# Weight, x, y and m tiles moved to multiples of 64 bytes in a hybrid-mixer and FFN kernel

## The chip, the cores and the metric

The kernel runs on one core of a Trainium2 chip, in one launch. The metric is the device time of that core in microseconds (us), the median of several runs. All times below come from those runs or from one execution taken by the hardware profiler.

## What is computed

Two blocks follow each other on one sequence of 256 tokens, 1024 wide, all in float32. The first has a mixer (an RG-LRU branch, a gated linear attention, a block attention with relative bias), then a SwiGLU FFN, each with RMS norms. The second has two layers, both modulated by a condition vector `c`: a short convolution with an FFN, then an attention with forget gates and an FFN. Cut to the part that fills the time:

```python
def first_block(x, ...):
    h = rms_norm(x, pre_mix_norm)
    x = x + rms_norm(hybrid_mixer(h, w_in, ...) @ w_out, post_mix_norm)
    h = rms_norm(x, pre_ffn_norm)
    f = (silu(h @ w_ffn_gate) * (h @ w_ffn_up)) @ w_ffn_down
    return x + rms_norm(f, post_ffn_norm)

def second_block(x, c, ...):
    for l in range(2):
        sh1, sc1, g1, sh2, sc2, g2 = split(silu(c) @ w_ada[l] + b_ada[l], 6)
        h = x * (1 + sc1) + sh1
        y = short_conv_mixer(h, ...) if l == 0 else forgetting_attention(h, ...)
        x = layer_norm(ALPHA * x + g1 * y, ...)
        h = x * (1 + sc2) + sh2
        y = (silu(h @ w_gate[l]) * (h @ w_up[l])) @ w_down[l]
        x = layer_norm(ALPHA * x + g2 * y, ...)
    return x
```

The widths are 1024 for the model and 2816 (22 tiles of 128) inside the FFNs.

## The kernel before

**Layout.** Activations are kept transposed: a tile is 128 features on the partitions by 256 tokens along the row, and the 1024 features are NK = 8 such k tiles. Weights come as blocks of 128 x 128; eight blocks make one `raw` tile of 1024 columns, loaded by one 512 KB transfer on the SP queue (`raw_load`).

**Two halves.** TensorE multiplies in fp32r. To keep float32's accuracy every operand is split in two: a rounded high part and the rest as a low part. For weights `weights` does it (ScalarE writes `wh`, L140; VectorE writes `wl`, L144), for operands `hilo`, `modulate`, `deep_norm` and the end of `evac` in `ffn`. Each product is then three matmuls: high by high, low weight by high operand, high weight by low operand (`mm3`, L151 to L153). The weight block is the stationary operand, the operand tile of 256 columns the moving one.

**The operand tiles.** `hl_tiles` makes the x tiles (`xh`, `xl`) and the y tiles (`yh`, `yl`), eight of each kind in pools that live through the whole program. They are T + 2 = 258 columns wide: in `lazy` two further columns, for the scale and shift of a layer norm, go through the same matmuls, and everywhere else only the first 256 are used. The m tiles (`mh`, `ml`, the inner values of an FFN, 22 of each) are made in `ffn` (L888, L889), also 258 columns wide, of which the first 256 are used.

**Order of the matmuls.** `single` and `pair` go over k inside one output tile: three matmuls on k tile 0, three on k tile 1, and so on (`mm3`). `ksteps` (L186 to L192, under `kouter`, `partial` and `lazy`) goes over k outside: one x or y high tile meets four to eight weight blocks in a row, high and low weight in turn, then its low tile meets the high weights. A down projection (`single` with 22 k tiles) does the same as other singles over m tiles. `tokmajor` (L240 to L242) has the operand as the stationary side and 256 or 512 weight columns as the moving one, and `small_proj` (L468, L469) uses 16 or 32 columns of a small weight tile `w_glrs` or `w_fs`.

**What sets the order.** A scheduler places the instructions of each engine by a simulated timeline, bound by the dependencies that `after` adds. `fill` puts a share of the 112 modulation products (`gemv`, a 512 KB transfer and one VectorE instruction each, L360) between the projections.

**Where tiles lie.** Pools are laid out one behind the other along the row of a partition; a tile's row is rounded up to a multiple of 32 bytes, so 258 columns of 4 bytes, 1032, take 1056. The first pool, `const`, holds the constants made in `consts`; behind it come `raw`, `whp`, `wlp`, `gp`, `xp` and the rest.

The placing lines before:

```python
w = T + 2                                              # hl_tiles, L247
h = self.tl(pool or self.xp, [P, w], tag + "h", F32R, NK)
h = self.tl(self.fp, [P, T + 2], "mh", F32R)[:, 0:T]   # ffn, L888
```

Of the kernel before, what the change touches and what calls it, by code (L numbers as in the profile page):

```python
# [10 lines left out]
F32R = mybir.dt.float32r  # L11
# [6 lines left out]
P = 128  # L18
D = 1024
T = 256  # L20
# [43 lines left out]
class Net:  # L64
# [42 lines left out]

    def ms(self, shape=(P, 512)):
        return self.tl(self.pms, list(shape), "ms")

    def acc(self, shape=(P, 512)):
        return self.tl(self.pacc, list(shape), "acc")
# [131 lines left out]

    def hl_tiles(self, tag, pool=None):

        w = T + 2  # L247
        h = self.tl(pool or self.xp, [P, w], tag + "h", F32R, NK)
        l = self.tl(pool or self.xp, [P, w], tag + "l", F32R, NK)
        return h, l, h[:, 0:T], l[:, 0:T]  # L250

    def hilo(self, src, tag="x", scale=None, pool=None):
# [126 lines left out]
    def consts(self):  # L379
        nc, cp, a = self.nc, self.cp, self.a  # L380
        self.vt = self.tl(cp, [P, NVEC], "vec")
        nc.scalar.dma_start(self.vt, a["vec"])
        self.x0 = []
        self.early = []
        for i in range(NK // 2):
            t = self.tl(self.sp, [P, 2, T], "ax", bufs=NK // 2)
            nc.sync.dma_start(t, a["xT"][i])
            self.x0 += [t[:, 0, :], t[:, 1, :]]
            if i < EARLY:
                self.early.append(self.raw_load(i, 4 if i == 0 else 2))  # L390
        self.ct = self.tl(cp, [P, NCST], "cst")
        nc.sync.dma_start(self.ct, a["cst"])
        self.odim = self.tl(cp, [P, P], "odim")
        nc.gpsimd.memset(self.odim, 1.0 / D)
        self.rdim = self.tl(cp, [P, 1], "rdim")
        nc.vector.memset(self.rdim, 1.0 / D)
        self.ident = self.tl(cp, [P, P], "ident")
        make_identity(nc, self.ident)
        self.tbl = self.tl(cp, [P, 1], "tbl")
        nc.vector.memset(self.tbl, 0.0)  # L400
        nc.scalar.activation(self.tbl, self.tbl, AF.Exp)
        self.G = self.tl(cp, [P, T], "fG", BF16)
        nc.gpsimd.memset(self.G, 0.0)
        self.fsel = self.tl(cp, [P, 16], "fsel", BF16)
        nc.gpsimd.memset(self.fsel, 0.0)
        for o in (0, 32, 64):
            nc.vector.tensor_copy(self.fsel[o:o + 16, :], self.ident[o:o + 16, o:o + 16])
        self.fneg = self.tl(cp, [P, 16], "fneg", BF16)
        nc.vector.tensor_scalar(self.fneg, self.fsel, -1.0, None, ALU.mult)
        self.identb = self.tl(cp, [P, P], "identb", BF16)  # L410
        nc.vector.tensor_copy(self.identb, self.ident)
        self.cmask = self.tl(cp, [P, P], "cmask", BF16)
        cm = self.tmp("p_sq")[:, 0:P]
        nc.gpsimd.memset(cm, 0.0)
        nc.gpsimd.affine_select(out=cm, in_=cm, compare_op=ALU.is_ge, fill=NEG, base=0,
                                pattern=[[-1, P]], channel_multiplier=1)
        nc.vector.tensor_copy(self.cmask, cm)
        self.gmask = self.tl(cp, [P, P], "gmask")
        nc.gpsimd.memset(self.gmask, 1.0)
        nc.gpsimd.affine_select(out=self.gmask, in_=self.gmask, compare_op=ALU.is_ge, fill=0.0, base=0,  # L420
                                pattern=[[1, P]], channel_multiplier=-1)
        nc.gpsimd.memset(self.gmask[0:64, 64:128], 0.0)
        self.hmask = self.tl(cp, [P, 4], "hmask")
        nc.gpsimd.memset(self.hmask, 0.0)
        self.bmask = self.tl(cp, [P, 4, 64], "bmask")
        nc.gpsimd.memset(self.bmask, 0.0)
        for h in range(4):
            nc.gpsimd.memset(self.hmask[32 * h:32 * h + 32, h:h + 1], 1.0)
            nc.gpsimd.memset(self.bmask[32 * h:32 * h + 32, h, :], 1.0)
        self.hsel = self.tl(cp, [P, 2], "hsel")  # L430
        nc.gpsimd.memset(self.hsel, 0.0)
        for h in range(2):
            nc.gpsimd.memset(self.hsel[64 * h:64 * h + 64, h:h + 1], 1.0)
        self.resetm = self.tl(cp, [P, 4, 64], "resetm")
        nc.gpsimd.memset(self.resetm, 1.0)
        nc.gpsimd.memset(self.resetm[:, :, 0:1], 0.0)
        cst = lambda name, n, rows=P: self.ct[0:rows, COFF[name]:COFF[name] + n]
        self.rel = cst("rel_bias", 8, 32)
        self.oh = cst("onehot", T, 32)
        self.gw2 = cst("gate_w2", P, 32)  # L440
        self.fold = cst("fold", 16, 32)
        self.bf = cst("b_f", 1, 16)
        self.wbd = [cst(n, 2 * P).rearrange("p (t c) -> p t c", t=2) for n in ("lru_wa", "lru_wx")]
        self.wsm = []
        for name in ("w_glr", "w_f"):
            r = cst(name, P).rearrange("p (k c) -> p k c", k=NK)
            w = self.tl(cp, [P, NK, 2, 16], name + "s", F32R)
            nc.scalar.activation(w[:, :, 0, :], r, AF.Copy)
            nc.vector.tensor_tensor(w[:, :, 1, :], r, w[:, :, 0, :].bitcast(F32), ALU.subtract)
            self.wsm.append(w)  # L450
        self.ada = self.tl(cp, [P, 112], "ada")

    def silu_c(self):
        nc, ca = self.nc, self.a["c"]
        self.cact = self.tl(self.cp, [P, D], "cact")
        cb = self.tl(self.gp, [P, D], "gw")
        nc.sync.dma_start(cb, bass.AP(tensor=ca.tensor, offset=ca.offset, ap=[[0, P], [1, D]]))
        nc.scalar.activation(self.cact, cb, AF.Tanh, scale=0.5)
        nc.vector.scalar_tensor_tensor(cb, self.cact, 1.0, cb, op0=ALU.add, op1=ALU.mult)
        nc.vector.tensor_scalar(self.cact, cb, 0.5, None, ALU.mult)  # L460
# [408 lines left out]
    def ffn(self, l, X, R=None, R2=None, first=(), rows=None):  # L869

        nc = self.nc
        V = nc.vector
        MH, ML = [], []

        def evac(g, u):
            if R is not None:
                g2 = self.tmp("ff_g")
                V.tensor_tensor(g2, g, R, ALU.mult)
                u2 = self.tmp("ff_u")
                V.tensor_tensor(u2, u, R2, ALU.mult)  # L880
                s = self.silu2(g2)
                m = self.tmp("ff_m")
                V.tensor_tensor(m, s, u2, ALU.mult)
            else:
                s = self.silu2(g)
                m = self.tmp("ff_m")
                V.scalar_tensor_tensor(m, s, 0.5, u, op0=ALU.mult, op1=ALU.mult)  # L887
            h = self.tl(self.fp, [P, T + 2], "mh", F32R)[:, 0:T]  # L888
            lo = self.tl(self.fp, [P, T + 2], "ml", F32R)[:, 0:T]  # L889
            nc.scalar.activation(h, m, AF.Copy)  # L890
            V.tensor_tensor(lo, m, h.bitcast(F32), ALU.subtract)
            MH.append(h)
            ML.append(lo)

        wg, wu = f"g{l}", f"u{l}"
        n = len(first) // 2
        for j in range(n):
            evac(*[self.lazy_out(first[2 * j + q], *rows, self.tmp("ff_g" if q == 0 else "ff_u")) for q in range(2)])
        for ps in self.kouter([(w, n + j) for j in range(4) for w in (wg, wu)], X, R is None):
            evac(ps[:, 0, :], ps[:, 1, :])  # L900
        for j in range(n + 4, NFF):
            ps = self.pair(wg, j, wu, j, X)
            self.drain()
            evac(ps[:, 0, :], ps[:, 1, :])
        return MH, ML
# [530 lines left out]
```

## Time and profile before

| | us |
|---|---|
| runs before, median of 3 | 1001.16 (1000.77 to 1001.65) |
| the profiled execution | 1001.6 |
| its span, first to last instruction | 999.9 |
| TensorE (PE) busy | 933.7 (93%) |
| weight loads (PEld) busy, beside PE | 900.9 (90%) |
| VectorE (DVE) busy | 809.8 (81%) |
| ScalarE (ACT) busy | 525.7 (53%) |
| GpSimd (POOL) busy | 20.3 (2%) |
| mean granted TensorE clock | 0.97 of 2.4 GHz |
| HBM traffic | 220 GB/s, 219.57 MB in all |

A busy share is an average over the whole span. The profile gives a matmul the time from its start until its last result, which overlaps the next one; the distance between the starts of two matmuls is what each of them costs in a dense stretch, and it is read from the timeline, or as the length of a stretch over the count of its instructions. Starts are given to 0.01 us, so a distance is read over many matmuls.

### The profile page before, as it was taken

The numbers are of one execution on the slowest core, as the hardware profiler recorded it, in microseconds if no ns is written. First come the engines' busy times: TensorE is split into PE (matmuls) and PEld (weight loads), VectorE is DVE, ScalarE is ACT, GpSimd is POOL, SyncE is SP. The second block draws the span as 40 slices with busy tenths as digits, with TensorE's granted clock in tenths as the row PEclk, the third lists the DMA queues.
The fourth block names the chain that finished last, engine by engine and source line by source line (L and its number), as shares of the span: only waits on it lengthen the run. The fifth ranks groups of instructions, "written<-read, shape, count | busy, mean of one in ns | idle before, by whom it ended". The sixth has DMA issues, their size and how long they took to land.

```text
span 999.9 us, 19159 instructions
## 1 busy us (share of the span) xinstructions
PE 933.7 (93%) x7430; PEld 900.9 (90%) x7430; DVE 809.8 (81%) x1584; ACT 525.7 (53%) x941; POOL 20.3 (2%) x66
## 2 busy tenths in 40 slices
PE   7989988999999799995899999999899889999996
PEld 7879888999999699995899999987798879999995
DVE  8887587999988788779999989889675898866554
ACT  7474554454444354456554445478455575545441
POOL 1111000000000000000000000000000000000001
PEclk9999999999999899997899999999999989999999
DMA  8753346888889667655779999854642447556541
GB/s 306 237 180 109 106 149 221 272 296 289 268 316 410 245 211 227 216 169 189 252 276 328 341 330 344 298 170 151 208 140 72 141 138 254 184 190 190 187 129 43
DMA packets 62347, 219.57 MB, mean 220 GB/s; under 512 B 7112, under 2 KB 8784, under 8 KB 62256
## 3 DMA queue, kind: packets, MB, share of 16 engines
q1 hardware_dynamic: 61056, 215.06, 63.1%
q0 software_dynamic: 1056, 3.16, 1.1%
q8 instruction: 58, 0.95, 0.4%
q14 instruction: 33, 0.27, 0.1%
q10 hardware_dynamic: 144, 0.13, 0.0%
HBM read 217.26 MB, written 2.63 MB: 220 GB/s over the span
## 4 chain that ended last, share of the span: by engine, by line
PE 78%; DVE 13%; issue 4%; ACT 3%; DMA 1%; POOL 0%; DVEq 0%; ACTq 0%; POOLq 0%
PE acc L151 19%; PE acc L153 19%; PE acc L152 18%; PE acc L186 4%; PE acc L187 4%; DVE wl L144 4%; PE acc L192 4%; DVE gw L360 3%; ACT wh L140 1%; PE ms L790 1%; DMA gw<-ada 1%; PE acc L189 1%; PE lg L743 1%; DVE yl L256 1%; PE acc L242 1%
## 5 line engine op out<-in xcount | busy, mean ns | idle before, releaser
L140 ACT ACTIVATE wh<-raw 128x1024 fp32r<-128x1024 f32 (+2 forms) x296 | 307.9, 1047 | 262.3 <-PE acc L153 138.0
L144 DVE TENSOR_TENSOR wl<-raw,wh 128x1024 fp32r<-128x1024 f32 (+2 forms) x296 | 357.2, 1210 | 91.2 <-ACT wh L140 89.0
L151 PE MATMUL acc<-yh,wh 128*128 128x256 f32 x608 | 170.4, 281 | 0.7 <-DVE ff_m L887 0.7
L153 PE MATMUL acc<-yl,wh 128*128 128x256 f32 x608 | 170.7, 281 | 0.0
L152 PE MATMUL acc<-yh,wl 128*128 128x256 f32 x608 | 170.2, 280 | 0.0
L151 PE MATMUL acc<-xh,wh 128*128 128x256 f32 x576 | 164.0, 285 | 5.9 <-DVE ff_u L880 4.1
L153 PE MATMUL acc<-xl,wh 128*128 128x256 f32 x576 | 163.1, 283 | 0.0
L152 PE MATMUL acc<-xh,wl 128*128 128x256 f32 x576 | 162.9, 283 | 0.0
L152 PE MATMUL acc<-mh,wl 128*128 128x256 f32 x528 | 148.4, 282 | 0.5 <-DVE wl L144 0.5
L153 PE MATMUL acc<-ml,wh 128*128 128x256 f32 x528 | 147.9, 281 | 0.0
L151 PE MATMUL acc<-mh,wh 128*128 128x256 f32 x528 | 147.8, 281 | 0.0
L360 DVE SCALAR_TENSOR_TENSOR gw<-gw,cact 128x1024 f32<-128x1024 f32 x112 | 135.4, 1222 | 3.6 <-DMA gw<-ada 3.5
L151 PEld LDWEIGHTS acc<-xh,wh 128*128 128x128 f32 x576 | 110.0, 191 | 7.6 <-DVE ff_u L880 4.3
L151 PEld LDWEIGHTS acc<-yh,wh 128*128 128x128 f32 x608 | 114.7, 189 | 0.9 <-issue 0.9
L152 PEld LDWEIGHTS acc<-yh,wl 128*128 128x128 f32 x608 | 114.8, 189 | 0.4 <-issue 0.4
L153 PEld LDWEIGHTS acc<-yl,wh 128*128 128x128 f32 x608 | 114.5, 188 | 0.6 <-issue 0.6
L152 PEld LDWEIGHTS acc<-xh,wl 128*128 128x128 f32 x576 | 110.1, 191 | 0.4 <-issue 0.3
L153 PEld LDWEIGHTS acc<-xl,wh 128*128 128x128 f32 x576 | 109.8, 191 | 0.0
L152 PEld LDWEIGHTS acc<-mh,wl 128*128 128x128 f32 x528 | 99.4, 188 | 0.7 <-DVE wl L144 0.7
L153 PEld LDWEIGHTS acc<-ml,wh 128*128 128x128 f32 x528 | 99.5, 189 | 0.0
L151 PEld LDWEIGHTS acc<-mh,wh 128*128 128x128 f32 x528 | 99.1, 188 | 0.0
L186 PE MATMUL acc<-xh,wh 128*128 128x256 f32 (+1 forms) x256 | 69.0, 296 | 7.8 <-ACT wh L140 5.5
(403 smaller groups left out, 1568.2 us busy)
## 6 DMA issues: line engine op xcount, KB each, us to landing
raw<-wts SPq DMA_DIRECT2D x288, 512.0 KB, 4.3
gw<-ada SPq DMA_DIRECT2D x112, 512.0 KB, 5.2
raw<-wts SPq DMA_DIRECT2D x6, 256.0 KB, 5.6
m_scr<-m_row POOLq DMA_DIRECT2D x2, 768.0 KB, 5.8
ax<-xT SPq DMA_DIRECT2D x4, 256.0 KB, 4.6
m_b<-m_scr POOLq DMA_DIRECT2D x8, 128.0 KB, 3.4
out<-fg SPq DMA_DIRECT2D x8, 128.0 KB, 1.8
cst<-cst SPq DMA_DIRECT2D x1, 588.5 KB, 7.0
```

Of the source, the lines that this page charges most:

```text
L140: i = nc.scalar.activation(self.wh[:, d], r, AF.Copy)
L144: self.anchor = nc.vector.tensor_tensor(self.wl[:, d], r, self.wh[:, d].bitcast(F32), ALU.subtract)
L151: m = [mm(ps, wh, xh, start=start, stop=False), mm(ps, wl, xh, start=False, stop=False), mm(ps, wh, xl, start=False, stop=stop)]
L152: mm(ps, wl, xh, start=False, stop=False),
L153: mm(ps, wh, xl, start=False, stop=stop)]
L186: m.append(mm(outs[i], wh, X[0][k], start=k == 0 and i % per == 0, stop=False))
L187: m.append(mm(outs[i], wl, X[0][k], start=False, stop=False))
L189: m.append(mm(outs[i], wh, X[1][k], start=False, stop=i % per == per - 1))
L192: m.append(mm(outs[i], wh, X[1][k], start=False, stop=False))
L242: mm(outs[tt], h, wl, start=False, stop=k == NK - 1 and (tt == 1 or not one))
L256: self.lo = self.nc.vector.tensor_tensor(l, src, h.bitcast(F32), ALU.subtract)
L360: i = nc.vector.scalar_tensor_tensor(t, t, 1.0, self.cact, op0=ALU.mult, op1=ALU.mult, accum_out=self.ada[:, g:g + 1])
```

## The change

Three edits of placement. `shift` takes 8 columns (32 bytes) in the `const` pool, as a tile that is written once and never read; all pools behind it move by 32 bytes. The x and y tiles become T + 16 = 272 columns wide, 1088 bytes, with the same 258 columns in use. The m tiles become 256 columns wide, 1024 bytes.

```diff
+    def shift(self, pool, n):
+
+        if n:
+            self.nc.gpsimd.memset(self.tl(pool, [P, 8 * n], "pad", bufs=1), 0.0)
+
...
     def hl_tiles(self, tag, pool=None):
 
-        w = T + 2
+        w = T + 16
         h = self.tl(pool or self.xp, [P, w], tag + "h", F32R, NK)
         l = self.tl(pool or self.xp, [P, w], tag + "l", F32R, NK)
+        h, l = h[:, 0:T + 2], l[:, 0:T + 2]
         return h, l, h[:, 0:T], l[:, 0:T]
...
         self.ada = self.tl(cp, [P, 112], "ada")
+        self.shift(cp, 1)
...
-            h = self.tl(self.fp, [P, T + 2], "mh", F32R)[:, 0:T]
-            lo = self.tl(self.fp, [P, T + 2], "ml", F32R)[:, 0:T]
+            h = self.tl(self.fp, [P, T], "mh", F32R)
+            lo = self.tl(self.fp, [P, T], "ml", F32R)
```

Where the tiles begin in the two built programs, as the byte in a partition's row modulo 512 (the x and y tiles in the order k = 0 to 7; the y tiles have the same remainders as the x tiles):

| tiles | before | with the change |
|---|---|---|
| raw, wh, wl (all twelve) | 352 | 384 |
| xh, yh | 352, 64, 32, 0, 480, 448, 416, 384 | 384, 320, 256, 192, 128, 64, 0, 448 |
| xl, yl | 96, 320, 288, 256, 224, 192, 160, 128 | 384, 320, 256, 192, 128, 64, 0, 448 |
| mh (22, two layouts) | all sixteen multiples of 32 | 384 throughout |
| ml (22, two layouts) | all sixteen multiples of 32 | 384 throughout |
| w_glrs, w_fs (small projections) | 448 | 448 |

A weight block inside `wh` or `wl` begins a multiple of 512 bytes behind the tile's start, so the remainder of the tile holds for every block.

On TensorE, ScalarE and the SP queue the instructions stand in the same order in both programs. On VectorE and POOL a few rows at the start differ. VectorE before, from the last constants to the second x tile's low part (`xl` is a low part of x, `lga` and `lba` columns for the layer norms, `cmask` the causal mask):

```order
L578 COPY g_z_474<-vec_90 128x2
L503 TENSOR_SCALAR nb_494<-vec_90 128x2
L504 TENSOR_SCALAR nb_494<-vec_90 128x2
L417 CAST cmask_139<-p_sq_140 128x128
L682 TENSOR_SCALAR g_gh_819<-vec_90 128x2
...
L259 SCALAR_TENSOR_TENSOR xl_181<-ax_92,vec_90,xh_180 128x256
L1315 TENSOR_SCALAR lga_1910_9832<-vec_90 128x8
L1317 TENSOR_SCALAR lba_1911_9834<-vec_90 128x8
L259 SCALAR_TENSOR_TENSOR xl_185<-ax_92,vec_90,xh_184 128x256
L144 TENSOR_TENSOR wl_239<-raw_94,wh_238 128x256 x4
```

and with the change:

```order
L423 CAST cmask_139<-p_sq_140 128x128
L585 COPY g_z_476<-vec_90 128x2
L510 TENSOR_SCALAR nb_496<-vec_90 128x2
L511 TENSOR_SCALAR nb_496<-vec_90 128x2
L689 TENSOR_SCALAR g_gh_821<-vec_90 128x2
...
L1322 TENSOR_SCALAR lga_1911_9834<-vec_90 128x8
L265 SCALAR_TENSOR_TENSOR xl_183<-ax_92,vec_90,xh_182 128x256
L1324 TENSOR_SCALAR lba_1912_9836<-vec_90 128x8
L265 SCALAR_TENSOR_TENSOR xl_187<-ax_92,vec_90,xh_186 128x256
L149 TENSOR_TENSOR wl_241<-raw_94,wh_240 128x256 x4
```

The cast of the mask has moved up by three rows, and the first `lga` ahead of the first `xl`; what stands before the first `wl` is the same set. POOL with the change, at the same place (`pad` is the new tile, `m_T` a tile for the relative bias, `p_sq` the mask before its cast):

```order
L437 MEMSET hsel_162 128x2
L441 MEMSET resetm_166 128x256
L114 MEMSET pad_176 128x8
L421 AFFINE_SELECT p_sq_140<-p_sq_140 128x128
L832 MEMSET m_T_386 8x384
L515 MEMSET l_xpad_499 128x3
```

Before, the memset of `m_T` stood where that of `pad` stands now.

## Rows read from the trace of the kernel before

**Rows 1.** The page: TensorE's busy time, and the chain that ended last

```profile
PE 933.7 (93%) x7430; PEld 900.9 (90%) x7430; DVE 809.8 (81%) x1584; ACT 525.7 (53%) x941; POOL 20.3 (2%) x66
...
PE 78%; DVE 13%; issue 4%; ACT 3%; DMA 1%; POOL 0%; DVEq 0%; ACTq 0%; POOLq 0%
```

**Rows 2.** Stretches: length, busy (count) of PE, PEld, DVE, ACT, POOL, clock, DMA, GB/s

```profile
175.00:275.00 100.00, 100.00 (x853) 100.00 (x852) 93.84 (x164) 48.33 (x70) 0.00 (x0) 1.00 0.84 282
...
500.00:575.00 75.00, 75.00 (x639) 75.00 (x639) 71.98 (x129) 39.46 (x67) 0.00 (x0) 1.00 0.89 315
...
575.00:645.00 70.00, 70.00 (x592) 70.00 (x591) 62.38 (x100) 32.60 (x44) 0.00 (x0) 1.00 0.92 333
...
850.00:925.00 75.00, 75.00 (x640) 75.00 (x639) 54.01 (x80) 38.73 (x58) 0.00 (x0) 1.00 0.59 188
```

**Rows 3.** TensorE, logits of the attention: start, time from start to result, bf16 matmuls

```profile
711.14 0.27 PE L750 MATMUL lg<-fG,fneg 80*128 80x256 bf16 x1
711.25 0.22 PE L749 MATMUL lg<-fsel,fG 80*128 80x128 bf16 x1
```

**Rows 4.** TensorE, 512 columns in tokmajor, first and last of thirteen starts

```profile
41.95 0.39 PE L240 MATMUL acc<-wh,xh 128*128 128x512 f32 x1
...
44.73 0.39 PE L240 MATMUL acc<-wh,xh 128*128 128x512 f32 x1
```

**Rows 5.** TensorE, small projection, first and fifteenth start

```profile
33.83 0.28 PE L468 MATMUL ms<-xh,w_glrs 128*32 128x256 f32 x1
...
35.47 0.28 PE L151 MATMUL acc<-xh,wh 128*128 128x256 f32 x1
```

**Rows 6.** Whole span, instructions of L151, of L186 and of L192

```profile
0.00:999.90 999.90, 482.22 (x1712) 323.87 (x1712) 0.97 0.65 220
...
0.00:999.90 999.90, 138.24 (x512) 102.84 (x512) 0.97 0.65 220
...
0.00:999.90 999.90, 72.09 (x448) 62.58 (x448) 0.97 0.65 220
```

**Rows 7.** TensorE, convolution's k-outer stage, k = 0: first and ninth start

```profile
347.47 0.28 PE L186 MATMUL acc<-xh,wh 128*128 128x256 f32 x1
...
348.43 0.28 PE L192 MATMUL acc<-xl,wh 128*128 128x256 f32 x1
```

**Rows 8.** TensorE, first FFN's k-outer stage, k = 6: first and fifteenth start

```profile
155.25 0.28 PE L186 MATMUL acc<-xh,wh 128*128 128x256 f32 x1
...
156.90 0.28 PE L192 MATMUL acc<-xl,wh 128*128 128x256 f32 x1
```

**Rows 9.** TensorE, `wo` partial sums, y tile of k = 6: first and seventh start

```profile
768.85 0.28 PE L187 MATMUL acc<-yh,wl 128*128 128x256 f32 x1
...
769.53 0.28 PE L187 MATMUL acc<-yh,wl 128*128 128x256 f32 x1
```

**Rows 10.** TensorE, first FFN's k-outer stage, k = 3: first and seventeenth start

```profile
145.98 0.28 PE L186 MATMUL acc<-xh,wh 128*128 128x256 f32 x1
...
147.88 0.28 PE L192 MATMUL acc<-xl,wh 128*128 128x256 f32 x1
```

**Rows 11.** TensorE, convolution's k-outer stage, k = 5: first and seventeenth start

```profile
360.77 0.28 PE L186 MATMUL acc<-xh,wh 128*128 128x256 f32 x1
...
362.69 0.29 PE L192 MATMUL acc<-xl,wh 128*128 128x256 f32 x1
```

**Rows 12.** Start of the program, a row each of POOL, VectorE and TensorE

```profile
2.00 0.10 POOL L424 MEMSET hmask<- 128x4 f32 x1
...
5.36 0.17 DVE L1315 TENSOR_SCALAR lga<-vec 128x8 f32<-128x8 f32 x1
...
6.38 0.58 PE L187 MATMUL acc<-xh,wl 128*128 128x256 f32 x1 [0.28 <-DVE wl L144]
```

**Rows 13.** VectorE by form: count, busy us and mean ns, idle time before

```profile
L144 DVE TENSOR_TENSOR wl<-raw,wh 128x1024 fp32r<-128x1024 f32 x290 | 354.3, 1224 | 90.5 <-ACT wh L140 88.3
...
L891 DVE TENSOR_TENSOR ml<-ff_m,mh 128x256 fp32r<-128x256 f32 x66 | 27.6, 423 | 0.1
```

## The prediction, made before the change was run

> **What bounds the kernel now.** I read the page first: its busy shares and its chain, then stretches of the trace, then single matmuls. TensorE is busy 93% of the span and carries 78% of the chain that ended last [rows 1]. In four long stretches where it never stops the granted clock is 1.00, which is the 2.4 GHz level, so what counts there is the distance from one matmul's start to the next [rows 2]. With x tiles it is 100 us / 853 = 117.2 ns, with y tiles 75 / 639 = 117.4 and 75 / 640 = 117.2, with the m tiles of the second FFN's down projection 70 / 592 = 118.2. (A window also counts a matmul or two that began before it, so the true gaps are some 0.3 ns larger.)
>
> The gap has room in it. The same 256 columns in bf16 take 0.11 us [rows 3]; so 256 columns can pass in some 109 ns, and the fp32r stream is 8 ns slower. It is no fixed cost per matmul: with 512 columns the twelve gaps from 41.95 to 44.73 are 231.7 ns each [rows 4], twice 116. It is not the next weight load either: in the small projection, which loads only 32 or 16 columns of weights, the fourteen gaps from 33.83 to 35.47 are still 117.1 [rows 5]. So the moving stream itself is slow, by about 7%, at full clock.
>
> How many matmuls does that touch? L152 and L153 have as many as L151, L187 as many as L186, so 3 x 1712 + 2 x 512 + 448 = 6608 [rows 6]. At 117.5 ns they are 776 us, which is the chain's 78%. **One ns per matmul is 6.6 us.** That is the only lever of this change.
>
> **Does the place of the operands matter at all?** In a k-outer stage one high tile is the moving side of eight to sixteen matmuls in a row, and the placement table says where each stood. "Relative" is the moving tile's byte minus the weight tile's, modulo 128.
> - Relative 0 (352 and 352): eight gaps from 347.47 to 348.43, 120.0 ns each [rows 7].
> - Relative 64 (416 and 352): fourteen gaps from 155.25 to 156.90, 117.9 [rows 8]; but in another chain with the same relation six gaps from 768.85 to 769.53, 113.3 [rows 9].
> - Relative 32 (0 and 352), moving tile at a multiple of 64: sixteen gaps from 145.98 to 147.88, 118.8 [rows 10].
> - Relative 96 (448 and 352), again at a multiple of 64: sixteen from 360.77 to 362.69, 120.0 [rows 11].
>
> The reader is to see two things. The gaps do depend on place or history, by up to 6%. And a moving tile at a multiple of 64 is no better than one 32 bytes off: 118.8 and 120.0 against 117.9, 113.3 and 120.0. The weights give no such comparison, since they lie 32 bytes off in every full-width matmul of the kernel before; only the small projection's weight tile starts at a multiple of 64, and there the gap is 117.1 with both kinds of x tile in turn.
>
> The Trainium skill (TensorE: Matmul & The Clock Gate, Step-by-step: what each phase is for) says that TensorE has two independent read ports and that loading the next weights takes nothing from the running matmul; by it the weights' place is worth 0 us, where by the chains it could be worth 120.0 - 113.3 = 6.7 ns a matmul. The Trainium skill (SBUF — State Buffer, Specifications (TRN2)) gives SBUF lines of 16 bytes; multiples of 32 and of 64 both start a line, so by that rule the whole change is worth 0 us, and the five chains, which differ without any order by 64, neither prove nor break it.
>
> **The change part by part.**
> 1. *The pad's memset* on POOL: the nearest row is a 128x4 memset of 0.10 us, at 2.0 us of the span [rows 12]. It takes the place of a longer memset that moves behind the next instruction, so what VectorE waits for there comes no later. VectorE's start is on the path: TensorE's second matmul waits for the first wl split, 0.28 us [rows 12]. But the same eighteen rows stand before that split in both orders, two of them swapped or moved up; the 128x8 instruction that now runs ahead of the first x split took 0.17 us with its pipeline [rows 12]. 0 us; were nothing hidden, 0.1 + 0.17, some 0.3 us.
> 2. *VectorE and ScalarE*: a wl split of 1024 columns takes 1224 ns, an ml split of 256 columns 423 [rows 13]. The difference is 801 / 768 = 1.04 ns a column, though the first reads three tiles that are all 32 off and the second has its tiles on either kind of place. A cost per column from the placement would show as a spread here; I put 0. Were it 1% of VectorE's work, 0.9 us of the 93.84 in the first stretch, it would lie under TensorE there, and in the other three, where VectorE is at 72 to 96% [rows 2].
> 3. *Loads*: the same 512 KB per raw tile, landing 32 bytes further on. The DMA engines are the bound in no stretch of rows 2, with shares of 0.59 to 0.92. 0 us.
> 4. *x and y matmuls*, 6608 - 1584 = 5024 (22 x 8 x 3 m matmuls in each of three FFNs) [rows 6]: before, the eight k tiles pass relative 0, 96, 64 and 32 twice over; now 0 and 64 alternate. By the chains the four cost (120.0 + 120.0 + 117.9 + 118.8) / 4 = 119.2 and the two that are left (120.0 + 117.9) / 2 = 119.0. That is -0.2 ns x 5024 = -1.0 us. I take 117.9 for relative 64 because its chain is the longer one; with 113.3 the two sums are 118.0 and 116.7, -1.3 ns or -6.5 us. The other end is a lock on 120.0 in the relative-0 half alone: (120.0 - 117.5) x 2512 = +6.3 us.
> 5. *m matmuls*, 1584: before, h and l tiles pass through all four relations; now every m tile, high and low, is at the same byte modulo 512 as the weights, relative 0 throughout. By the chains 120.0 against 119.2, +0.8 x 1584 = +1.3 us. Lower end: the m stretches become as fast as the y stretches, whose high and low tiles have also been at equal relation, 117.2 - 118.2 = -1.0 ns, -1.6 us. Upper end: 120.0 against the 118.5 they have now, +2.4 us.
>
> Sum: -1.0 + 1.3 = +0.3 us on the profiled execution's 1001.6, which is 1001.9; that execution is 0.4 above the median of the runs, so **1001.5 us**. The mechanism behind this forecast: the stream is slow for a reason that a shift by 32 bytes leaves alone, and only the mix of relations changes a little. Its own range, with 0.6 ns a matmul either way, is 997 to 1006.
>
> **The rivals.**
> *Full alignment pays.* A weight tile and a moving tile that both begin at a multiple of 64 never met in a full matmul before. If a read that begins inside a 64-byte stretch costs a beat, it goes away now. The price that the trace shows is the fastest chain, 113.3: (117.5 - 113.3) x 6608 = 27.8 us, so 973; half of it, 987. If the stream came down to bf16's 109, it would be 8.5 x 6608 = 56 us and 945, but VectorE is busy 93.84 of 100 and 71.98 of 75 us in two of the stretches [rows 2], so there only 4 to 6% can be had and 950 to 960 is nearer. For it: the 113.3 chain shows that 117.5 is no floor. Against it: that chain had both operands 32 off, and the small projection with an aligned weight tile gained nothing.
>
> *A lock on the slow rhythm.* At relative 0 the chain of rows 7 ran at exactly 120.0 on average. The m tiles now sit there for whole projections of 66 matmuls each, and half of the x and y tiles do. Price: 1.5 x 1584 + 2.5 x 2512 = 2.4 + 6.3 = 8.7 us, 1010. It decides as soon as relative 0 costs more than 118.5 in the m stretches. Against it: an x or y tile meets only three matmuls in a row in most stages, perhaps too few to fall into a rhythm.
>
> That the change does not do what it says can be set aside: in the built program every raw, wh, wl, x, y and m tile begins at a multiple of 64.
>
> **How the numbers follow.** 0.2% is 2 us, about what a measurement can tell. The forecast has 0.35: most of it within 2 us (0.28), the rest on both sides. Full alignment, in whole or in part, has 0.38; I give it that much because its one decisive combination is untested, and about 0.10 of it lies below 978. The lock has 0.27, with 0.08 above 1008 and 0.01 too small to see. So faster 0.41, same 0.29, slower 0.30, and the range is 978 to 1008.
>
> **What would show it.** Right: in the same stretches 117 to 118 ns per matmul for x and y and 118 to 120 for m, VectorE's 1224 and 423 ns unchanged, TensorE's share 93%. Full alignment: 113 ns or less in both kinds of stretch, more idle time of TensorE behind VectorE. The lock: 120 in the m stretches, steady. A change in the waits or in the granted clock instead of the gaps would make the whole account wrong.

## The result and the profile after

| | before | with the change |
|---|---|---|
| median of the runs, us | 1001.65 (1000.77 to 1003.54) | 1008.25 (1005.41 to 1010.3) |
| ratio, 95% interval | | 1.0061 [1.0048, 1.0074] |
| profiled execution, its span, us | 1001.6, 999.9 | 1005.41, 1003.7 |

The change costs 0.6%, some 6 us. The profiled execution is the fastest of its five, so its span understates that; what follows rests on the distances between matmuls, not on the span.

The page of the changed kernel, engine totals and chain, beside [rows 1]:

```profile
PE 934.7 (93%) x7430; PEld 901.9 (90%) x7430; DVE 809.7 (81%) x1584; ACT 525.9 (52%) x941; POOL 20.7 (2%) x67
...
PE 80%; DVE 12%; ACT 4%; issue 3%; DMA 0%; DVEq 0%; ACTq 0%
```

Nothing else took over: the engines' work is the same, and TensorE carries 80% of the chain instead of 78%. The same four stretches as in [rows 2] (length, busy time and count of PE, PEld, DVE, ACT, POOL, then the granted clock, DMA share, GB/s):

```profile
175.00:275.00 100.00, 100.00 (x843) 100.00 (x842) 93.13 (x162) 47.81 (x69) 0.00 (x0) 1.00 0.84 278
...
500.00:575.00 75.00, 75.00 (x633) 75.00 (x632) 72.11 (x131) 39.66 (x69) 0.00 (x0) 1.00 0.90 314
575.00:645.00 70.00, 70.00 (x586) 70.00 (x586) 62.92 (x102) 33.09 (x45) 0.00 (x0) 1.00 0.93 335
850.00:925.00 75.00, 75.00 (x633) 75.00 (x632) 53.24 (x79) 38.24 (x56) 0.00 (x0) 1.00 0.61 188
```

TensorE is again never idle there and the clock is again 1.00. What differs is the count: 843 for 853, 633 for 639 and 640, 586 for 592. One per cent fewer matmuls pass in the same time, with x, y and m tiles alike.

The m stretch of the second FFN in the changed kernel's timeline (start, time to the result, engine, line), the first two of 71 starts and the last:

```profile
599.79 0.28 PE L157 MATMUL acc<-mh,wl 128*128 128x256 f32 x1
599.91 0.28 PE L158 MATMUL acc<-ml,wh 128*128 128x256 f32 x1
...
608.19 0.28 PE L157 MATMUL acc<-mh,wl 128*128 128x256 f32 x1
```

70 gaps in 8.40 us: 120.0 ns, and not on average only. Of 1575 gaps between m matmuls in the whole trace 1466 read exactly 120 ns. The table reads both traces in the same way: it takes every distance under 130 ns between two starts of the same kind (a longer one nearly always holds a wait) and puts its mean on all matmuls of that kind.

| mean distance of two starts, ns | before | with the change | matmuls | worth, us |
|---|---|---|---|---|
| m (`mm3`) | 118.90 | 119.97 | 1584 | +1.7 |
| x and y in `mm3` | 117.54 | 118.86 | (608 + 576) x 3 = 3552 | +4.7 |
| x and y in `ksteps`, 256 columns | 118.22 | 117.57 | 1104 | -0.7 |
| x and y in `ksteps`, 258 columns (`lazy`) | 120.24 | 120.53 | 432 | +0.1 |

The sum is +5.8 us, inside the measured 4.8 to 7.4.

VectorE's two forms of [rows 13], in the changed kernel:

```profile
L149 DVE TENSOR_TENSOR wl<-raw,wh 128x1024 fp32r<-128x1024 f32 x290 | 353.2, 1220 | 93.5 <-ACT wh L145 91.5
...
L898 DVE TENSOR_TENSOR ml<-ff_m,mh 128x256 fp32r<-128x256 f32 x66 | 27.2, 418 | 0.3
```

1220 for 1224 and 418 for 423 ns: VectorE gains nothing worth naming from tiles at multiples of 64.

The other engines do not set the gap either. Of the changed kernel's m gaps 145 fell where neither VectorE nor ScalarE ran; their mean is 119.9 ns, and where both ran throughout it is 120.0. The m stretches of the second and third FFN have the same count, though the DMA engines are busy for 0.96 of the one and 0.55 of the other:

```profile
600.00:640.00 40.00, 40.00 (x336) 40.00 (x335) 37.40 (x59) 20.03 (x27) 0.00 (x0) 1.00 0.96 358
...
935.00:975.00 40.00, 40.00 (x336) 40.00 (x335) 22.81 (x29) 16.16 (x19) 0.00 (x0) 1.00 0.55 169
```

### The profile page after: what moved, and what is told of

Same layout as the page of the kernel before. It is cut to its first block, busy times and chain, and to the rows that moved or that the text cites. A ratio compares the mean times of both kernels' runs of the same rounds, so it can differ in the third digit from the quotient of the medians.

```text
span 1003.7 us, 19161 instructions
## 1 busy us (share of the span) xinstructions
PE 934.7 (93%) x7430; PEld 901.9 (90%) x7430; DVE 809.7 (81%) x1584; ACT 525.9 (52%) x941; POOL 20.7 (2%) x67
## 3 DMA queue, kind: packets, MB, share of 16 engines
q0 software_dynamic: 1056, 3.16, 1.1%
## 4 chain that ended last, share of the span: by engine, by line
PE 80%; DVE 12%; ACT 4%; issue 3%; DMA 0%; DVEq 0%; ACTq 0%
PE acc L156 20%; PE acc L158 19%; PE acc L157 19%; PE acc L191 4%; PE acc L192 4%; PE acc L197 4%; DVE wl L149 4%; DVE gw L366 2%; ACT wh L145 1%; PE ms L797 1%; PE lg L750 1%; PE acc L194 1%; DVE yl L262 1%; PE acc L247 1%; PE acc L246 1%
```

## The experiments

"Relation" is the moving tile's byte minus the weight tile's, modulo 512 where no other modulus is named. Gaps are mean distances between starts in the profiled execution, taken as in the table above. Each run has one profiled execution.

### Which part of the change costs

**e1_shift_only** keeps the pad alone, **e2_widths_only** the widths alone, **e3_m_only** and **e4_xy_only** one width each. Against the changed kernel, e1 reads

```diff
-        w = T + 16
+        w = T + 2
...
-            h = self.tl(self.fp, [P, T], "mh", F32R)
-            lo = self.tl(self.fp, [P, T], "ml", F32R)
+            h = self.tl(self.fp, [P, T + 2], "mh", F32R)[:, 0:T]
+            lo = self.tl(self.fp, [P, T + 2], "ml", F32R)[:, 0:T]
```

and e2 leaves out `self.shift(cp, 1)`. e3 has no pad and only the new m width, e4 no pad and only the new x and y width.

> Only the 32-byte pad: every tile moves by 32 bytes, so the weights begin at multiples of 64 while x, y and m keep their 258 columns and every relation between weights and moving tiles stays as before. Theory A (the gap depends on the relation of moving and weight tile modulo 128, not on multiples of 64): same as before within 0.2%, gaps 117.5 ns for x and y and 118.9 for m, with the same rhythm in the k-outer chains. Theory B (the absolute place counts, aligned weights are the cost): gaps move towards those of the changed kernel, 118.8 and 120, and the time rises by 4 to 8 us. Theory C (aligned weights help and the widths hurt): faster by over 2 us.

> The widths 272 and 256 without the pad: all tiles are 32 bytes off a multiple of 64, the relations are those of the changed kernel. Theory A: as slow as the changed kernel, +6 to +8 us (1.006 to 1.008), m gaps 120.0 and x and y gaps 118.8. Theory B: no slower than before by more than 2 us.

> Only the m tiles 256 columns wide: all m tiles at relation 0. Theory A: m gaps 120.0 instead of 118.9, 1584 x 1.1 ns = +1.7 us, x and y unchanged at 117.5. Theory B: no change of the gaps.

> Only the x and y tiles 272 columns wide: their relations alternate between 0 and 64, m keeps all relations. Theory A: x and y gaps 118.8 instead of 117.5, 5024 x 1.3 ns = +6.5 us, m unchanged at 118.9; with the run before it the two add up to the whole change. Theory B: no change of the gaps.

| | us | ratio to before | gap m | gap x, y in `mm3` |
|---|---|---|---|---|
| e1, pad only | 1002.0 | 1.0003 [0.9994, 1.0012] | 118.90 | 117.54, 117.55 |
| e2, widths only | 1007.42 | 1.0057 [1.0043, 1.007] | 119.98 | 118.84, 118.86 |
| e3, m width only | 1003.38 | 1.0013 [1.0002, 1.0023] | 119.96 | 117.54 |
| e4, x and y widths only | 1006.71 | 1.0047 [1.0035, 1.0059] | 118.89 | 118.82, 118.87 |

Stretches of e1, with x, m and y tiles:

```profile
175.00:275.00 100.00, 100.00 (x853) 100.00 (x852) 93.72 (x163) 48.19 (x71) 0.00 (x0) 1.00 0.84 280
575.00:645.00 70.00, 70.00 (x592) 70.00 (x592) 63.63 (x104) 33.52 (x46) 0.00 (x0) 1.00 0.94 341
850.00:925.00 75.00, 75.00 (x640) 75.00 (x639) 53.44 (x80) 38.86 (x57) 0.00 (x0) 1.00 0.63 189
```

The same of e2:

```profile
175.00:275.00 100.00, 100.00 (x843) 100.00 (x843) 93.18 (x162) 47.81 (x69) 0.00 (x0) 1.00 0.83 276
575.00:645.00 70.00, 70.00 (x587) 70.00 (x586) 63.43 (x102) 32.44 (x45) 0.00 (x0) 1.00 0.95 340
850.00:925.00 75.00, 75.00 (x633) 75.00 (x632) 54.26 (x83) 39.31 (x58) 0.00 (x0) 1.00 0.63 187
```

And e3's stretch with m tiles, then e4's with x tiles:

```profile
575.00:645.00 70.00, 70.00 (x588) 70.00 (x587) 63.64 (x102) 32.51 (x46) 0.00 (x0) 1.00 0.95 341
```

```profile
175.00:275.00 100.00, 100.00 (x843) 100.00 (x843) 93.16 (x162) 47.84 (x69) 0.00 (x0) 1.00 0.84 279
```

In e1 every raw and weight tile moves by 32 bytes with all pools behind it, the weights come to a multiple of 64, and the counts are those of before to the matmul: 853, 592, 640. e2 has the weights 32 off and, to within one, the counts of the changed kernel. So **the multiple of 64 is worth nothing, and the widths alone cost what the whole change costs**: they set how moving tiles lie against the weights. e2 beside the changed kernel is also the test of full alignment: the same relations, once with weight and moving tiles 32 off, once with both on multiples of 64, take 1.0057 and 1.0061. The parts add up: 0.13% + 0.47% = 0.60%. The gaps are those of theory A in all four runs; its times for e2 and e4, 6 to 8 and 6.5 us, were somewhat too high (5.7 and 4.7).

### The relation itself, with the widths of the change kept

**e5_after_gap64** is the changed kernel with 64 bytes put between the weights and the operand tiles:

```diff
         self.shift(cp, 1)
+        self.shift(self.gp, 2)
```

The m tiles go from relation 0 to 64; the x and y tiles keep their spacing, and the even and odd ones change places.

> The changed kernel with 64 bytes more between the weight tiles and all tiles behind them: every tile still begins at a multiple of 64 and the steps from one moving tile to the next stay; only the relation to the weights moves by 64, for m from 0 to 64 throughout, for x and y the halves at 0 and 64 swap. Theory A1 (relation of moving tile to weight tile): m leaves its 120.0 ns for a rhythm of relation 64, 113.3 or 117.9, so 1584 x (2 to 6.7) = 3 to 10 us faster than the changed kernel; x and y stay near 118.8. Theory A2 (only the step between consecutive moving tiles counts, 0 in m): m stays at 120.0 and the time is that of the changed kernel, 1.006.

Measured: 1004.45 us, ratio 1.0028 [1.0017, 1.0039]. Its timeline in the second FFN, a start and the eighteenth after it:

```profile
610.04 0.28 PE L156 MATMUL acc<-mh,wh 128*128 128x256 f32 x1
...
612.16 0.28 PE L156 MATMUL acc<-mh,wh 128*128 128x256 f32 x1
```

2.12 us / 18 = 117.8 ns; over all m matmuls 117.78, in place of 119.97. The spacing from one m tile to the next is still a multiple of 512 and all tiles still begin at multiples of 64: what has changed is the distance to the weights. That e1 moved weights and operands together by 32 bytes without effect says that it is not the operand's place in the row either. The m gaps where neither VectorE nor ScalarE ran, 146 of them, are at 117.8 too.

The x and y gaps in `mm3` stay at 118.83 and 118.87, and tile by tile they show more than that. Sorted by the relation of the moving tile modulo 256 (its k follows from the order, eight k tiles to a projection):

| relation modulo 256 | 0 | 64 | 128 | 192 |
|---|---|---|---|---|
| changed kernel, ns | 118.19 | 117.55 | 120.41 | 119.22 |
| e5, ns | 118.18 | 117.55 | 120.41 | 119.24 |
| before, ns | 117.16 | 116.71 | 119.10 | 117.46 |

In e5 each relation belongs to the next tile in the order, and its gap has gone there with it. Theory A2, by which the steps alone count, is out for x and y as for m. But before, where tiles are 1056 bytes apart instead of 1088, the same relations cost 0.8 to 1.8 ns less: what runs next to a tile counts as well.

### Other relations

**f1_rel64** and **f2_rel32** have no pad in `const`, x and y tiles 288 columns apart, and a pad ahead of the m tiles of each FFN. f1 against the changed kernel:

```diff
-        w = T + 16
+        w = 288
...
-        h, l = h[:, 0:T + 2], l[:, 0:T + 2]
+        h, l = h[:, 16:16 + T + 2], l[:, 16:16 + T + 2]
...
-        self.shift(cp, 1)
...
+        self.shift(self.fp, (2, 6, 14)[l])
```

x and y lie at 64, 192, 320 and 448, m at 64, 192 and 448 in FFN 0, 1 and 2. f2 begins the tiles 8 columns in and takes `(1, 3, 4)`: x and y at 32, 160, 288 and 416, m at 32, 96 and 128.

> No pad in front; x and y tiles 1152 bytes apart and begun 64 bytes in, so that every one has relation 64 to the weights modulo 128; m tiles at relation 64, 192 and 448 (all 64 modulo 128) in the three FFNs. Theory A1: every matmul has the good relation; gaps 117.7 at worst, so 1.000, and 113.3 at best, 6608 x 4.2 = 28 us faster than before, 0.972. Theory A2: the steps are 0 and multiples of 128, gaps 118.8 to 120, slower by 5 to 15 us.

> As the run before, with x and y at relation 32 modulo 128 and the m tiles of the three FFNs at 32, 96 and 128. Theory A1: m at 128 runs at 120.0 as at relation 0, m at 32 and 96 at other steady gaps, between 116 and 121, which the windows of the three down projections show apart; x and y 117 to 119. Theory A2: all three down projections have the same gap, since the step is 0 in each.

f1 took 997.53 us, ratio 0.9952 [0.9936, 0.9967], f2 1002.26, 1.0009 [0.9993, 1.0026]. In f2 the m gaps were 120.0 at 96, 118.7 at 128 and 117.3 in the mean at 32, where FFN 0 began at 116.7 and, after a wait of 0.67 us, ran at 117.8. f1 lies between the bounds of A1 and not where A2 had it. That f2's three differ speaks against A2 again; that 128 is not at the 120.0 of 0 is a miss of A1, whose relation is modulo 128. f1's m stretches in FFN 1 and FFN 2:

```profile
600.00:640.00 40.00, 40.00 (x342) 40.00 (x341) 38.29 (x62) 20.06 (x28) 0.00 (x0) 1.00 0.96 349
...
935.00:975.00 40.00, 40.00 (x355) 40.00 (x355) 24.35 (x32) 16.31 (x20) 0.00 (x0) 1.00 0.49 145
```

342 and 355 in 40 us, both at full clock: 117.8 and 113.3 ns in the timeline, at relations 192 and 448, which are the same modulo 128 and modulo 256. So either the modulus is larger, or something besides the relation decides. The next three kernels ask that.

**g0_m448** is f1 with `(14, 14, 14)`, so that m lies at 448 in all three FFNs. **g1_m448_xy320** is g0 with x and y tiles 320 columns apart, begun 48 columns in: relations 192 and 448 only. **g2_sweep** is g1 with an offset of 56 columns (224 and 480) and `(10, 8, 15)`: m at 320, 256 and 480.

> The kernel of f1_rel64 with one edit: the m tiles of all three FFN layers lie 448 bytes behind the weight tile modulo 512, where f1 had 64, 192 and 448 in FFN 0, 1 and 2. In f1's trace the m matmuls of FFN 2 followed each other every 113.6 ns, those of FFN 0 and 1 every 117.6 to 118.2. Theory C (the relation modulo 512 sets the rhythm, and 448 is a better one than 64 and 192): FFN 0 and 1 come to 113.6 too, 1056 matmuls x 4.2 ns = 4.4 us less than f1's 997.5, so 993.1 us (ratio 0.991 to before), and 614 to 618 matmuls start between 575 and 645 us instead of 597. Theory A, as so far held (only the relation modulo 128 counts; FFN 2 was quick for a reason of its stage): no change against f1, 997.5, ratio 0.995, 597 in that window.

> As g0, and the x and y tiles are 320 columns apart and begun 48 columns in, so that they lie at 192 and 448 from the weights modulo 512, where f1 and g0 have 64, 192, 320 and 448. In f1's trace x and y high halves took 116.1 ns at 192 and 448, 118.2 at 64 and 320; low halves 116.0 to 116.9 and 118.4 to 119.1. Theory C: all x and y come to 116.2, 1.1 ns x 5024 = 5.5 us less than g0, so 987.6 us (ratio 0.986) if g0 is at 993.1; if a run of equal relations lets them lock as FFN 2's m did, up to 3.6 ns x 5024 = 18 us less, 975. Theory A (modulo 128): x and y unchanged, the time is that of g0. In the window 175 to 275 us: 861 to 880 matmuls under C, 852 under A.

> As g1, with relations not tried yet: m at 320, 256 and 480 in FFN 0, 1 and 2, x and y at 224 and 480. Theory A (modulo 128): m at 256 is as at 0, 120.0 ns (583 matmuls from 575 to 645 us), m at 320 as at 64, 117.8 ns, m at 480 and x and y as at 96, 120.0 for m and some 117.4 to 120 for x and y: some 1002 to 1010 us. Theory C gives no number for relations that were not run; it only says that 256 need not be as 0, nor 320 as 64, since 448 was not as 64 and 192.

g0: 996.23 us, ratio 0.9935 [0.992, 0.9951]. Its m stretches in FFN 1 and FFN 2:

```profile
600.00:640.00 40.00, 40.00 (x342) 40.00 (x341) 38.21 (x62) 20.10 (x28) 0.00 (x0) 1.00 0.96 355
...
935.00:975.00 40.00, 40.00 (x356) 40.00 (x355) 24.07 (x32) 16.93 (x20) 0.00 (x0) 1.00 0.47 146
```

FFN 1 did not become faster at 448: 342 again. Neither theory had that: 448 is not a quick relation, it is one at which two rhythms are possible. The first FFN of g0 shows the passage from one to the other (timeline; in brackets the idle time ahead and what ended it):

```profile
292.00 0.28 PE L156 MATMUL acc<-mh,wh 128*128 128x256 f32 x1
...
293.65 0.28 PE L158 MATMUL acc<-ml,wh 128*128 128x256 f32 x1
...
294.76 0.38 PE L157 MATMUL acc<-mh,wl 128*128 128x256 f32 x1 [0.60 <-DVE wl L149]
...
295.34 0.28 PE L158 MATMUL acc<-ml,wh 128*128 128x256 f32 x1
...
297.95 0.28 PE L157 MATMUL acc<-mh,wl 128*128 128x256 f32 x1
```

Fourteen gaps from 292.00 to 293.65 are 117.9 ns each. Then TensorE waits 0.60 us for a weight split. From 295.34 to 297.95 twenty-three gaps are 113.5 each, and the faster rhythm lasts until, at 326.85, four matmuls of another kind come between. The m matmuls behind them are slow again, fourteen gaps of 117.9:

```profile
328.83 0.28 PE L156 MATMUL acc<-mh,wh 128*128 128x256 f32 x1
...
330.48 0.28 PE L158 MATMUL acc<-ml,wh 128*128 128x256 f32 x1
```

Same tiles, same relation, same lines; only a pause or other matmuls lie between.

g1: 991.53 us (987.56 to 994.75), ratio 0.9889 [0.9868, 0.9911], the fastest kernel of this study and 1.1% ahead of before. Its stretches with x tiles, y tiles and m tiles:

```profile
180.00:270.00 90.00, 90.00 (x797) 90.00 (x796) 86.67 (x151) 45.34 (x65) 0.00 (x0) 1.00 0.88 295
...
500.00:570.00 70.00, 70.00 (x597) 70.00 (x596) 67.58 (x123) 35.33 (x61) 0.00 (x0) 1.00 0.94 333
600.00:640.00 40.00, 40.00 (x341) 40.00 (x341) 35.73 (x58) 18.91 (x25) 0.00 (x0) 1.00 0.91 330
```

With x 797 in 90 us (113.3 in steady stretches), with y 597 in 70 (117.8). Over the trace x in `mm3` ran at 113.9 and y at 117.1, though both lie at 192 and 448. So theory A (the time of g0) is out, and C, which gave 116.2 to x and y alike, is right on the gain alone. The runs of g1 spread over 7.2 us where those of before in the same session spread over 2.4; that fits rhythms that come out otherwise in each execution, but only one execution was profiled, so it isn't shown.

g2: 1006.47 us, ratio 1.0043 [1.0028, 1.0057]. Its second FFN, m at 256:

```profile
600.00:640.00 40.00, 40.00 (x335) 40.00 (x335) 37.76 (x60) 19.62 (x28) 0.00 (x0) 1.00 0.95 350
```

120.0 ns, in 526 of 527 gaps exactly: 256 is as slow and as steady as 0. m at 320 took 117.8, as at 64; at 480 it took 118.3, not the 120.0 of 96. x and y at 224 and 480 took 118.3. Theory A had the first two of these and the total, and missed at 480. So modulo 128 is not the whole rule, and relations 256 apart went alike in m wherever both were run (0 and 256, 64 and 320; 192 was seen at 117.8 only, 448 at that and at 113.3).

### Sixteen bytes

**h1_rel208** and **h2_rel176** are g1 with the x and y tiles begun 4 columns later and earlier:

```diff
-        h, l = h[:, 48:48 + T + 2], l[:, 48:48 + T + 2]
+        h, l = h[:, 52:52 + T + 2], l[:, 52:52 + T + 2]
```

> As g1_m448_xy320, only the x and y tiles begin 16 bytes later: 208 and 464 from the weights modulo 512, where g1 has 192 and 448 and g2 had 224 and 480. In g1's trace a stretch of x, y or m runs either at 113.3 or at 117.8 ns from its first matmuls to its last; at 224 and 480 (g2) it was 118.3. Theory D (steps of 32 bytes or more decide, so 208 goes with 192): the time of g1, 987 to 995 us, and x and y gaps near 113.3 or 117.8. Theory E (16 bytes count): another rhythm; if it is that of 224, x and y gaps of 118.3, 2.3 to 2.7 ns x 5024 = 12 to 14 us above g1, some 1003 to 1006 us.

> As g1_m448_xy320, only the x and y tiles begin 16 bytes earlier: 176 and 432 from the weights modulo 512; at 160 and 416 (half of f2's x and y tiles) the gaps were 118.0 to 119.4. Theory D (steps of 32 bytes or more decide, so 176 goes with 160): x and y at 118.2, some 1003 us. Theory E (16 bytes count): another rhythm, between 113.3 and 120; no bound of its own. If 113.3 comes without 117.8, the runs lie closer together than g1's 987.6 to 994.8 and below 988.

h1 took 1000.33 us, ratio 0.9992 [0.9983, 1.0001], h2 1004.52, 1.0029 [1.0016, 1.0042]. The stretch with x tiles in h1:

```profile
180.00:270.00 90.00, 90.00 (x757) 90.00 (x757) 83.32 (x146) 44.10 (x65) 0.00 (x0) 1.00 0.83 281
```

757 against g1's 797: 119.1 ns at 208 and 464, and 119.2 in h2 at 176 and 432, where 192 and 448 between them gave 113.3. With y tiles h1 changed its rhythm too: its last y stretch ran at 116.7.

```profile
850.00:910.00 60.00, 60.00 (x516) 60.00 (x516) 44.61 (x68) 31.83 (x47) 0.00 (x0) 1.00 0.61 190
```

Neither 113.3 nor 117.8, the two rhythms of g1, was seen in a long x or y stretch of h1 or h2, and both kernels are slower than g1 by more than the intervals. Sixteen bytes decide, and the quick place is narrow: theory D is out in h1, and E's guess of 118.3 is not what came. h2, 1 ns and 1.5 us above what D gave for it, decides little between the two. h1's m stretches in FFN 1 and FFN 2, at 448 as in g0, came out the other way round:

```profile
600.00:640.00 40.00, 40.00 (x355) 40.00 (x355) 38.94 (x62) 20.21 (x29) 0.00 (x0) 1.00 0.97 357
...
935.00:975.00 40.00, 40.00 (x342) 40.00 (x341) 22.98 (x29) 16.91 (x20) 0.00 (x0) 1.00 0.52 158
```

FFN 1 is quick and FFN 2 slow here, FFN 1 slow and FFN 2 quick in g0. That takes away the support for a cause that lies in the stage.

## Why the prediction was right or wrong

**The outcome.** 1.0061 x 1001.16 is 1007.3 us: inside the range of 978 to 1008 by 0.7 us, outside the forecast's own 997 to 1006. That it lies inside is owed to the width of the range, which was made for the rivals, and not to the account behind 1001.5. No change was the forecast; the rival of the lock, which had 0.27, is what came, with its own sign of a steady 120 in the m stretches, at 1010 a little too dear.

**What bounds the kernel** held. The distance of the starts was the lever, the clock stayed at 1.00 in all four stretches, and terms 1 to 3 came to nothing: VectorE's 1220 and 418 ns, POOL's one instruction more, DMA shares of 0.61 to 0.93 against 0.59 to 0.92. The count of 6608 matmuls leaves out 64: the low tile at k = 7 has a line of its own (L189). With them it is 6672, and nothing turns on the 1%.

**Full alignment** got 0.38, more than any other case, and is out: e1 puts every weight tile on a multiple of 64 and is at 1.0003, and the changed kernel, where weight and moving tiles both sit there, is as slow as e2, where none does. What spoke against it, a chain of 113.3 ns with both operands 32 off, was evidence enough to give it less.

**Term 5, m.** The mechanism was right: at relation 0 throughout, the m tiles lock on 120.0. The chain of [rows 7] had shown that with eight gaps, and those of [rows 8] and [rows 11] had 64 and 96 as m showed them later, at 117.8 and 120.0. The size was forecast at +0.8 ns and measured at +1.07, 1.7 us instead of 1.3, because m before cost 118.90 and not the 119.2 of the four chains.

**Term 4, x and y, is the step that failed**: "By the chains the four cost ... 119.2 and the two that are left ... 119.0. That is -0.2 ns x 5024." Every chain came from a k-outer stage, where one high tile is the moving side of eight to sixteen matmuls in a row, but 3552 of the 5024 matmuls are in `mm3`, where the moving tile changes after two and after one. For `ksteps` at 256 columns the sign was right, 118.2 to 117.6. For the 3552 the level before was 117.54, which [rows 2] had shown as 117.2 to 117.4, 1.7 ns below the chains' 119.2, and that gap in the argument was passed over: an order of work that runs 1.7 ns below its four chains is not their mean. It rose by 1.3 ns to 118.86, +4.7 us instead of -1.0.

**The lock's price** was also put in the wrong place for x and y: 2.5 ns on the relative-0 half alone. In the changed kernel the `mm3` gaps at relation 0 modulo 128 are 119.3 and those at 64 are 118.4; before, tiles at 0 took 118.1 and tiles at 64 took 117.1. Both halves slowed. By the table in e5's part each half is two relations modulo 256 with gaps of their own, so modulo 128 was too small, and a relation's gap changes with the spacing of the tiles. The rival's doubt, that three matmuls on one tile are too few for a rhythm, does not hold: the rhythm runs on over the tiles. That 8.7 us came near the measured 6 rests on errors that cancel.

**The weights' part.** The prediction set the weight side aside because the small projection, with 16 or 32 columns of weights, still has 117.1 ns. That did not follow: in e5 only the distance to the weight tiles changes, and the m gaps change by 2.2 ns.

**The two rules.** In e5 64 bytes between weights and operands take 2.2 ns off the mean m gap, and e1 shows that moving both does nothing. The Trainium skill (TensorE: Matmul & The Clock Gate, Step-by-step: what each phase is for) has two independent read ports and a weight load that takes nothing from the running matmul; e5's 2.2 ns do not agree with the prediction's reading of it, that the weights' place is worth 0 us. The Trainium skill (SBUF — State Buffer, Specifications (TRN2)) gives lines of 16 bytes, which the prediction read as no difference between starts at multiples of 32 and of 64. e1's 1.0003 agrees with that; the 113.3 to 120.0 ns of these kernels, all but two of which keep every tile on a multiple of 32, are not explained by it.

**Left open:** by what mechanism the distance to the weights acts (a collision of the weight and the moving stream fits, but no run shows one, and the small projection's 117.1 with its short weight loads is not explained), what picks the rhythm after a pause, and why 113.3 is open to 448 (and to 192 with 448 in g1's x tiles) and was not seen at 64 and 320 in m stretches, though the k-outer chain of [rows 9] ran at it with a high tile at 64. No kernel changed the weight blocks' own spacing.

## What to carry to other kernels

Where a dense matmul stretch is the bound, look at the moving tile's byte against the weight tile's, not at alignment: pads and widths that change these distances moved this kernel between 991.5 and 1008 us, with the same instructions on TensorE. Try several distances in steps of 16 bytes, and beside the median read the count of matmuls in fixed windows, which shows in which stretch a few us are won. A count holds for the execution that was profiled: at 448 one m stretch ran at 113.3 ns in one kernel and at 117.8 in another. A gap measured in one order of the same matmuls must not be put on another order: check first that it reproduces what that order costs now.

## What the runs showed of the hardware

- m stretches at full clock and with one relation throughout keep one mean gap for 256 fp32r columns until they are interrupted: 113.3, 116.7, 117.8, 118.3, 118.7 or 120.0 ns.
- m matmuls by relation modulo 512: 0 and 256 120.0; 32 116.7, then 117.8; 64 and 320 117.8; 96 120.0; 128 118.7; 480 118.3; 192 117.8; 448 113.3 or 117.8.
- x and y matmuls in `mm3` by relation modulo 256, tiles 1088 bytes apart: 0 118.2, 64 117.6, 128 120.4, 192 119.2, the same to 0.1 ns in four kernels (the changed one, e2, e4 and e5); tiles 1056 bytes apart: 117.2, 116.7, 119.1 and 117.5 (before).
- A rhythm, once begun, lasted through every m stretch without a pause. g0 changed its own at a wait of 0.60 us and f2 at one of 0.67 us, h1 at a single gap of 0.16 us; g1's first FFN kept 113.3 over two gaps of 0.63 and 1.17 us.
- The clock had no part in it: 1.00 in every stretch whose count is compared here.
